# Reordered split matmuls and a cast-free modulated input in a two-layer hybrid backbone on one Trainium2 core

## The chip, the cores and the metric

The kernel runs on one core of one Trainium2 chip, in one launch. The core has TensorE (PE in the rows, its weight loads PEld), VectorE (DVE), ScalarE (ACT), GpSimd (POOL) and SyncE (SP), which issues the transfers. The metric is the device time of one launch in microseconds, lower is better.

## The reference

Two layers act on 256 latent and 256 context tokens with 1024 features. Each sub-layer normalises its input, scales and shifts it with a vector made from the conditioning (adaLN), runs a feed-forward network or a token mixer, and closes with a second normalisation over the residual sum. What matters here is

```
def _modulate(x, shift, scale):
    return (_ln(x) * (1.0 + scale) + shift).astype(x.dtype)
def _post_ln(x, y, g, b):
    z = ALPHA * x.astype(jnp.float32) + y.astype(jnp.float32)
    return (_ln(z) * g + b).astype(x.dtype)
def _ffn_sublayer(x, shift, scale, gate, w_in, w_out, g, b):
    a, u = jnp.split(_modulate(x, shift, scale) @ w_in, 2, axis=-1)
    y = (jax.nn.silu(a) * u) @ w_out
    return _post_ln(x, 0.5 * gate * y, g, b)
...
    for i in range(DEPTH):
        x = _ffn_sublayer(x, ...)            # and the context tokens
        h = _modulate(x, m[:, 3], m[:, 4])
        y, yc = even or odd mixer of h, hc   # odd: GLA, 4 heads, low-rank gate (16); HGRN2, 4 heads
        x = _post_ln(x, m[:, 5] * y, ...)
        x = _ffn_sublayer(x, ...)            # context too, unless it is the last layer
```

The hidden width of a feed-forward network is 2816. Layer 0 mixes with a Fourier transform and a long convolution (Hyena), layer 1 with two gated linear scans in chunks of 64. Everything is float32.

## The kernel before

**Tiles.** The 512 tokens are four tiles of 128: tiles 0 and 1 latent, 2 and 3 context. After the odd mixer only tiles 0 and 1 go on. A sub-layer's input lies in `hT`, transposed (features on the partitions), each value as a high and a low part in fp32r that together hold the float32 value. Weights are split likewise into whi and wlo (hi and lo where they lie in spare tiles). Every large product is three fp32r matmuls that add into one PSUM bank: high by high, high by low, low by high (`mm3`, L459 to L462). In the rows L460 is the first of the three, L461 has the low part of its left operand's partner or of the weight, L462 the other low part, depending on which operand is stationary.

**Weights.** Class `Stream` loads units of 512 KB with SP, casts the high part on ACT (L78) and subtracts for the low part on DVE (L79). `get()` hands out a unit and loads and splits two ahead of it; `split_to` splits up to a given unit at the place in program order where it stands. The order of each engine's instructions is the order of emission; nothing reorders them later.

**A close.** When a tile's output is complete, `close` runs: `post_ln` on DVE (gate, residual, statistics, z, x), `norm` (statistics on DVE, xn on ACT, L398), two sets of four transposes on PE (L411, tile ptr), and `to_hT` (L413) for each set g = 0, 1: four modulations into an fp32 tile hm, all four by DVE (L428) or all four by ACT (L430), then a cast of hm to the high part on ACT and a subtraction for the low part on DVE or POOL (both `split`, L226 and L227). These steps are a generator; `step`, `due` and `flush` advance it between the matmuls of the next tile or stage, at places set by numbers in the table `G0`. `tm_head` (L521) runs the first units of the next stage tile by tile while the last tiles still close. `tok_out` (L475) runs the output products; the last six units of a feed-forward output (`TAIL`) are done for one tile first, then for the other, so that the first tile's close lies under the second's matmuls.

**Start.** The first stage has an order of its own, the string `ORDER`; there `to_hT` reads the transposed input xT from SBUF, not ptr.

**Odd mixer.** `odd_mixer` (L1094) projects features with `fm_lat` (latent tokens only, tile ql) and `fm_unit` (L464), makes the low-rank gate as one such unit (tile pab, of which 32 rows are used), and runs `attend` (L1318): scores pF from products with 64 rows of contraction (L1331), a mask and a sum on DVE (am, L1342), then the output po from am (L1348) and from the states (L1351, 64 rows of contraction for GLA).

Of the kernel before, what the change touches and what calls it, by code (L numbers as in the profile page):

```python
# [9 lines left out]
F32 = mybir.dt.float32  # L10
# [118 lines left out]
def kernel(ctx: ExitStack, tc: tile.TileContext, a, out, stop=None):  # L129
# [283 lines left out]

    def to_hT(t, g, xn, l, m, pt=None, eng=None):

        s = t // 2
        if pt is None:
# [6 lines left out]
        for i in range(4):  # L424
            k = 4 * g + i
            sc, sh = modc[:, l, COL_OF[m + 1], s, k:k + 1], modc[:, l, COL_OF[m], s, k:k + 1]
            if eng[0]:
                dve.tensor_scalar(hm[:, i], pt[:, P * i:P * i + P], sc, sh, op0=ALU.mult, op1=ALU.add)  # L428
            else:
                act.activation(hm[:, i], pt[:, P * i:P * i + P], AF.Identity, bias=sh, scale=sc)  # L430
        yield
        dst = hT["all"][:, 4 * g:4 * g + 4, :, P * t:P * t + P]
        split(dst[:, :, 0], dst[:, :, 1], hm, gp if eng[1] else dve)
        yield

    pend = {}
# [26 lines left out]

    def fm_unit(o, view=lambda x: x):  # L464

        hi, lo = ws.get()
        for k in range(KD):
# [8 lines left out]
    def tok_out(lhs, nk, tiles, fill=None, tail=0, done=None, cuts=None, hmajor=False):  # L476


        cols = {t: [slice(0, 512), slice(512, 1024)] for t in tiles}
        if cuts:  # L480
            cols[tiles[-1]] = cuts
        y = {t: [PS("y")[:, 0:c.stop - c.start] for c in cols[t]] for t in tiles}

        def mm(t, w, k, i):
            hh, hl = lhs(k, t)
            c = cols[t][i]
            mm3(y[t][i], hh, hl, w[0][:, c], w[1][:, c], k == 0, k == nk - 1)

        for k in range(nk - tail):
            w = ws.get()  # L490
            for t in tiles:
                for i in range(len(cols[t])):
                    mm(t, w, k, i)
            if fill:
                fill(k)
        held = {}
        last = ws.pos + tail
        limit = last
        while limit < len(ws.units) and ws.units[limit][2]:
            limit += 1  # L500
        ks = range(nk - tail, nk)
        for n, t in enumerate(tiles if tail else ()):
            nc_ = range(len(cols[t]))
            for i, (h, k) in enumerate([(h, k) for h in nc_ for k in ks] if n or hmajor else [(h, k) for k in ks for h in nc_]):
                if k not in held:
                    held[k] = ws.get(limit)
                mm(t, held[k], k, h)
                if fill and i % 2 and i < 2 * len(ks):
                    fill(ks[i // 2])
            if done:  # L510
                done(t, y[t])
        return y

    def tm_mm(y, w, kp, t):

        for kk in range(2):
            k = 2 * kp + kk
            c = slice(512 * kk, 512 * kk + 512)
            x = hT[k][:, :, P * t:P * t + P]
            mm3(y, x[:, 0], x[:, 1], w[0][:, c], w[1][:, c], k == 0, k == KD - 1)  # L520

    def tm_head(tiles, done, n=1):

# [5 lines left out]
        for t in tiles:  # L529
# [4 lines left out]
            if nw:  # L534
                warm(nw)
            y = [PS("hd") for _ in range(n)]
            for u in range(4 * n):
                if u not in w:
                    w[u] = ws.get(limit)
                tm_mm(y[u // 4], w[u], u % 4, t)  # L540
                if u == g_(f"{k0}t{t}", 1) and todo:
                    run(todo)
                    todo = None
# [540 lines left out]

    def queue_odd():
        for f in range(17):
            ws.add(a["od_fm"][f], True, f < g_("SPN", 4), g_(f"qoi{f}", int(f in (1, 3, 4) or f > 5 and f % 2 == 1)))
# [6 lines left out]
    def odd_mixer():  # L1094
        ab_c = Q([P, 2, 2], name="abc")
        sy.dma_start(out=ab_c, in_=a["gla_a_b"])
        aup = H([32, 2, 256], name="aup")
        sy.dma_start(out=aup, in_=a["gla_up"])
        reset = []
        for d in range(2):  # L1100
# [20 lines left out]
        def fm_lat(n):  # L1121

            o = PS("ql")[:, 0:L]
            hi, lo = ws.get()
            for k in range(KD):
                x = hT[k][:, :, 0:L]
                mm3(o, hi[:, P * k:P * k + P], lo[:, P * k:P * k + P], x[:, 0], x[:, 1], k == 0, k == KD - 1)
            step(n)
            return o

# [19 lines left out]


        pab = PS("pab")
        fm_unit(pab)
        ab = H([32, T], name="ab")
        act.copy(ab, pab[0:32, :])
        E, U = [], []

        def gla_exp():
# [160 lines left out]
        def attend(j, tt):  # L1319
# [6 lines left out]
            for n, f, r, hd in lst:  # L1326
                for d in range(2):
                    qk, xx = QK[d, j], XX[d, j]
                    for c in (d, 1 - d):
                        kk = (qk if c == d else xx)[r, 1, f, P * tt:P * tt + P]  # L1330
                        pe.matmul(pa[d][n // 2][:, P * (n % 2) + 64 * c:P * (n % 2) + 64 * c + 64], lhsT=kk,  # L1331
                                  rhs=qk[r, 0, f, P * tt + 64 * c:P * tt + 64 * c + 64], start=True, stop=True)
            yield
            z = az[turn[0] % 2]
            turn[0] += 1
            for d in range(2):
# [6 lines left out]
            yield  # L1343
            yield
            po = [PS("po") for _ in range(nh // 2)]
            for n, f, r, hd in lst:
                oc = po[n // 2][:, P * (n % 2):P * (n % 2) + P]
                pe.matmul(oc, lhsT=am[:, P * n:P * n + P], rhs=v[tt][:, P * hd:P * hd + P], start=True, stop=False)  # L1348
                for d in range(2):
                    s = 0 if (d == 0) == (tt == 0) else 1  # L1350
                    pe.matmul(oc, lhsT=XX[d, j][r, 0, f, P * tt:P * tt + P], rhs=ST[d, j][r, s, f, :],  # L1351
                              start=False, stop=d == 1)
# [223 lines left out]
    def mixer_close(l, tiles, nxt):  # L1576
# [6 lines left out]
            return hT[k][:, 0, P * t:P * t + P], hT[k][:, 1, P * t:P * t + P]  # L1583

        def done(t, y):
            if t == tiles[-1]:
                ws.split_spare(ws.pos + g_(f"{k0}a", 3))
                flush()
            else:
                ws.split_spare(ws.pos + g_(f"{k0}A{t}", 0))  # L1590
                older.append(t - 1)
            if t == tiles[0]:
                key[0] = k0
# [9 lines left out]
        older = []  # L1603
        tok_out(lhs, KD, tiles, fill, KD, done, None, g_(f"{k0}h", 0))

    def dump_hT():
# [207 lines left out]
def lay_out(inputs):  # L1814
# [67 lines left out]
    o["gla_up"] = up  # L1882
# [29 lines left out]
```

## Time and profile before

| | us |
|---|---|
| median of 3 runs | 1823.25 (1817.42 to 1825.67) |
| profiled execution | 1824.63 |
| its span | 1822.80 |
| PE busy | 1744.2 (96%) |
| DVE busy | 1256.4 (69%) |
| ACT busy | 713.3 (39%) |
| POOL busy | 252.9 (14%) |

The profile is one execution. A row of the timeline gives start, duration, engine, line, operation, output and inputs by the program's names, shapes and count; in square brackets stands the engine's idle time just before, and what ended it. The view of waits adds such idle times by the waiting line and by what released it. The ends of matmuls are modelled, so in a run of matmuls the distance of their starts is the time that one takes.

### The profile page before, as it was taken

To read this page: it belongs to the slowest core of one execution; us is meant where nothing else is said; L and a number is where in the kernel's file an instruction comes from. 1 tells how busy PE (TensorE), PEld (TensorE's weight loads), DVE (VectorE), ACT (ScalarE), POOL (GpSimd) and SP (SyncE) were. 2 spreads that over 40 slices of the span, in tenths; PEclk is the share of its full clock that TensorE was granted. 3 is DMA by queue.
4 is the path that set the end of the run, shared out by engine and by line. 5 is a ranking of instruction groups with operands and counts; after the bars stand their busy time and mean duration, and the time that the engine had idled before them with its cause. 6 is when DMAs were issued, how large, how long until landed. Compare 5 with 4: busy or idle time off the path is not lost. (4 is left out here: it accounts for less than half of the span.)

```text
span 1822.8 us, 21896 instructions
## 1 busy us (share of the span) xinstructions
PE 1744.2 (96%) x8204; PEld 1414.9 (78%) x8204; DVE 1256.4 (69%) x1818; ACT 713.3 (39%) x1048; POOL 252.9 (14%) x273
## 2 busy tenths in 40 slices
PE   6999999998999999999999999999998999989998
PEld 5788888777766788888887788888877778767887
DVE  6788887676788677777477677733576594666755
ACT  5432233453323433323335423233355463444443
POOL 1223311011000111111001111111011241110000
PEclk9999999999999999999999999999999999889999
DMA  9645756653124055554655455435554223446664
GB/s 329 226 179 199 253 218 235 219 178 139 59 88 144 24 205 211 185 189 169 219 187 173 163 212 201 173 105 196 194 177 141 81 93 92 143 139 219 208 213 134
DMA packets 91498, 314.90 MB, mean 173 GB/s; under 512 B 10848, under 2 KB 11584, under 8 KB 91392
## 3 DMA queue, kind: packets, MB, share of 16 engines
q1 hardware_dynamic: 85952, 297.09, 47.0%
q0 software_dynamic: 4576, 15.91, 2.8%
q8 instruction: 64, 1.05, 0.2%
q10 hardware_dynamic: 864, 0.51, 0.1%
q14 instruction: 42, 0.34, 0.1%
HBM read 308.18 MB, written 4.24 MB: 171 GB/s over the span
## 5 line engine op out<-in xcount | busy, mean ns | idle before, releaser
L79 DVE TENSOR_TENSOR wlo<-raw,whi 128x1024 fp32r<-128x1024 f32 x332 | 415.3, 1254 | 321.6 <-ACT whi L78 321.4
L78 ACT CAST whi<-raw 128x1024 fp32r<-128x1024 f32 x332 | 346.8, 1051 | 338.5 <-PE y L462 122.8
L243 DVE SCALAR_TENSOR_TENSOR mt<-mraw,cb 128x1024 bf16<-128x1024 f32 x256 | 309.7, 1250 | 2.5 <-DMA mraw<-in_mod_w_dram 2.5
L462 PE MATMUL pu<-hT,wlo 128*128 128x512 f32 x576 | 224.7, 390 | 3.2 <-DVE wlo L79 3.2
L460 PE MATMUL pu<-hT,whi 128*128 128x512 f32 x576 | 225.7, 392 | 0.0
L461 PE MATMUL pu<-hT,whi 128*128 128x512 f32 x576 | 224.4, 390 | 0.0
L460 PE MATMUL pa<-hT,whi 128*128 128x512 f32 x480 | 187.8, 391 | 0.0
L462 PE MATMUL pa<-hT,wlo 128*128 128x512 f32 x480 | 187.1, 390 | 0.0
L461 PE MATMUL pa<-hT,whi 128*128 128x512 f32 x480 | 187.0, 390 | 0.0
L461 PE MATMUL y<-wlo,hh 128*128 128x512 f32 x468 | 183.2, 391 | 3.8 <-DVE wlo L79 3.8
L460 PE MATMUL y<-whi,hh 128*128 128x512 f32 x468 | 183.1, 391 | 0.0
L462 PE MATMUL y<-whi,hh 128*128 128x512 f32 x468 | 182.5, 390 | 0.0
L226 ACT CAST hh<-sa 128x256 fp32r<-128x256 f32 x120 | 42.8, 404 | 296.0 <-DVE sa L614 296.0
L227 POOL TENSOR_TENSOR hh<-sa,hh 128x256 fp32r<-128x256 f32 x120 | 86.3, 739 | 516.5 <-ACT hh L226 507.1
L462 PEld LDWEIGHTS pu<-hT,wlo 128*128 128x128 f32 x576 | 108.1, 188 | 26.6 <-DVE wlo L79 4.1
L460 PEld LDWEIGHTS pu<-hT,whi 128*128 128x128 f32 x576 | 108.1, 188 | 23.5 <-ACT hh L226 0.8
L461 PEld LDWEIGHTS pu<-hT,whi 128*128 128x128 f32 x576 | 108.2, 188 | 22.8 <-issue 0.5
L461 PEld LDWEIGHTS y<-wlo,hh 128*128 128x128 f32 x468 | 87.9, 188 | 24.9 <-DVE wlo L79 7.0
L460 PEld LDWEIGHTS pa<-hT,whi 128*128 128x128 f32 x480 | 90.1, 188 | 19.7 <-issue 0.9
L234 POOL TENSOR_TENSOR rstd<-rp,mhalf 128x1 f32<-128x1 f32 x42 | 35.4, 846 | 500.8 <-DVE rp L233 494.7
L462 PEld LDWEIGHTS pa<-hT,wlo 128*128 128x128 f32 x480 | 90.1, 188 | 18.8
L461 PEld LDWEIGHTS pa<-hT,whi 128*128 128x128 f32 x480 | 90.1, 188 | 18.5
(396 smaller groups left out, 3022.3 us busy)
## 6 DMA issues: line engine op xcount, KB each, us to landing
raw<-in_ffn_out_dram SPq DMA_DIRECT2D x154, 512.0 KB, 3.6
mraw<-in_mod_w_dram SPq DMA_DIRECT2D x144, 512.0 KB, 5.1
raw<-in_ffn_in_dram SPq DMA_DIRECT2D x120, 512.0 KB, 3.8
raw<-in_ffn_tm_dram SPq DMA_DIRECT2D x44, 512.0 KB, 4.2
raw<-in_od_fm_dram SPq DMA_DIRECT2D x17, 512.0 KB, 3.9
raw<-in_od_tm_dram SPq DMA_DIRECT2D x16, 512.0 KB, 3.3
raw<-in_ffn_head_dram SPq DMA_DIRECT2D x12, 512.0 KB, 4.3
raw<-in_ev_in_dram SPq DMA_DIRECT2D x12, 512.0 KB, 3.4
```

The costliest lines, as they stand in the source:

```text
L78: self.nc.scalar.copy(hi, w)
L79: self.nc.vector.tensor_tensor(lo, w, hi.bitcast(F32), op=ALU.subtract)
L226: act.copy(dst_hi, src)
L227: (lo_eng or dve).tensor_tensor(dst_lo, src, dst_hi.bitcast(F32), op=ALU.subtract)
L234: gp.tensor_tensor(dst, t, mhalf.to_broadcast([P, n]), op=ALU.pow)
L243: dve.scalar_tensor_tensor(H([P, D], BF16, "mt"), w, 1.0, cb[s], op0=ALU.mult, op1=ALU.mult, accum_out=acc[:, s, b:b + 1])
L460: pe.matmul(o, lhsT=wh, rhs=xh, start=start, stop=False)
L461: pe.matmul(o, lhsT=wh, rhs=xl, start=False, stop=False)
L462: pe.matmul(o, lhsT=wl, rhs=xh, start=False, stop=stop)
```

## The change

It has five parts.

1. The three products of a split matmul are no longer issued per k. `fm_unit`, `fm_lat`, `tok_out` (in blocks), `tm_mm` and `tm_head` issue a pass of high by high over all k (or units) first, then a pass with one low part, then a pass with the other. Their number is the same.
2. `to_hT` makes no cast. For each set of four columns one engine writes the modulated value straight into the fp32r high part (ACT for g = 0, DVE for g = 1), the other engine makes the same value in fp32 (hm), and DVE or POOL subtracts as before. Each of the 44 sets is thus modulated twice, eight instructions where there were four and a cast.
3. The low-rank gate (pab) takes its weight unsplit and runs as 16 fp32 matmuls of 32 columns that lie in four column groups, where 24 fp32r matmuls of 128 columns stood; the weight that follows is repeated four times to sum the groups.
4. `attend` issues its products so that those on the upper and the lower 64 rows stand next to each other and write different banks; for GLA there is no break between the scores and the mask.
5. The close of the odd mixer splits the next stage's weights during tile 0's output, by a list of unit numbers, not at the tiles' ends.

```
     def to_hT(t, g, xn, l, m, pt=None, eng=None):
...
+        dst = hT["all"][:, 4 * g:4 * g + 4, :, P * t:P * t + P]
+        def modulated(o, on_dve):
+            for i in range(4):
...
+                if on_dve:
+                    dve.tensor_scalar(o[:, i], pt[:, P * i:P * i + P], sc, sh, op0=ALU.mult, op1=ALU.add)
+                else:
+                    act.activation(o[:, i], pt[:, P * i:P * i + P], AF.Identity, bias=sh, scale=sc)
+        modulated(dst[:, :, 0], g)
+        yield
         hm = H([P, 4, P], name="hm")
...
-        split(dst[:, :, 0], dst[:, :, 1], hm, gp if eng[1] else dve)
+        modulated(hm, not g)
+        if not given:
+            yield
+        (gp if eng[1] else dve).tensor_tensor(dst[:, :, 1], hm, dst[:, :, 0].bitcast(F32), op=ALU.subtract)

     def fm_unit(o, view=lambda x: x):
-            mm3(o, hi[:, P * k:P * k + P], lo[:, P * k:P * k + P], view(hT[k][:, 0, :]), view(hT[k][:, 1, :]), k == 0, k == KD - 1)
+        for n, (a_, b_) in enumerate(((0, 0), (0, 1), (1, 0))):
+            for k in range(KD):
+                pe.matmul(o, lhsT=w[a_][:, P * k:P * k + P], rhs=view(hT[k][:, b_, :]), start=n + k == 0, stop=n == 2 and k == KD - 1)

     # tok_out
+        def block(todo):
+            for a_, b_ in ((0, 0), (1, 0), (0, 1)):
+                for t, w, k, i in todo:
+                    pe.matmul(y[t][i], lhsT=lhs(k, t)[a_], rhs=w[b_][:, cols[t][i]], start=k + a_ + b_ == 0, stop=k == nk - 1 and b_ == 1)

     # tm_mm (the first stage)
-            mm3(y, x[:, 0], x[:, 1], w[0][:, c], w[1][:, c], k == 0, k == KD - 1)
+            for n in range(2):
+                pe.matmul(y, lhsT=x[:, n], rhs=w[0][:, c], start=n + k == 0, stop=False)
+        for kk in range(2):
+            k = 2 * kp + kk
+            pe.matmul(y, lhsT=hT[k][:, 0, P * t:P * t + P], rhs=w[1][:, 512 * kk:512 * kk + 512], start=False, stop=k == KD - 1)

     # tm_head
+            order = ((0, 0), (1, 0), (0, 1)) if t == tiles[0] else ((0, 0), (0, 1), (1, 0))
+            for v in range(12 * n):
+                p_, u = divmod(v, 4 * n)

     # odd_mixer, pab
-        fm_unit(pab)
-        act.copy(ab, pab[0:32, :])
+        for n in range(2):
+            for k in range(KD):
+                j = k % 4
+                pe.matmul(pab[32 * j:32 * j + 32, :], lhsT=w[:, P * k:P * k + 32], rhs=hT[k][:, n, :].bitcast(F32),
+                          start=n == 0 and k < 4, stop=n == 1 and k >= 4, tile_position=(0, 32 * j))
+        act.copy(ab, pab)

     # mixer_close, fill(k)
+            if l and "y" not in seen:
+                ws.split_to(first + (4, 5, 7, 8, 9, 10, 11, 11)[k])
```

Three places in the order of instructions show what moves. The first is the start on DVE, where the modulation of the first tile's first set (hm from xT), the split of the first stage's second weight unit (lo from raw) and the low part of `hT` stand. Before:

```order
L1670 SCALAR_TENSOR_TENSOR modc<-pt_345,modb 128x2x4
L428 TENSOR_SCALAR hm_348<-xT_207,modc 128x128 x4
L79 TENSOR_TENSOR lo_354<-raw_164,hi_353 128x1024
L227 TENSOR_TENSOR hT_104<-hm_348,hT_104 128x4x128
L304 BN_STATS st_399<-x_175 128x6 x2
```

And now:

```order
L1717 SCALAR_TENSOR_TENSOR modc<-pt_345,modb 128x2x4
L79 TENSOR_TENSOR lo_353<-raw_164,hi_352 128x1024
L432 TENSOR_SCALAR hm_375<-xT_207,modc 128x128 x4
L442 TENSOR_TENSOR hT_104<-hm_375,hT_104 128x4x128
L304 BN_STATS st_402<-x_175 128x6 x2
```

The weight's subtraction has moved ahead of the modulation and of everything that follows it.

The second is ACT at the same place; modr is the row of conditioning that the first modulation waits for. Before:

```order
L1666 COPY modr_343<-pm_299 128x128
L78 CAST hi_353<-raw_164 128x1024
L226 CAST hT_104<-hm_348 128x4x128
L430 ACTIVATE hm_411<-xT_270,modc 128x128 x4
L226 CAST hT_104<-hm_411 128x4x128
```

And now:

```order
L1713 COPY modr_343<-pm_299 128x128
L434 ACTIVATE hT_104<-xT_207,modc 128x128 x4
L78 CAST hi_352<-raw_164 128x1024
L434 ACTIVATE hT_104<-xT_270,modc 128x128 x4
L226 CAST cf_102<-dft_231 128x256
```

The first set's high part is now written by ACT ahead of the weight's cast, for which DVE's subtraction waits.

The third is PE in `attend` for GLA, first token tile of the last pass: scores pF, products of the latent gate rc, outputs po. Before, one head's output and the next's:

```order
L1348 MATMUL po_12275<-vg_11879,am_12243 128x128
L1351 MATMUL po_12275<-st_12169,xx_11685 128x128
L1351 MATMUL po_12275<-st_12184,xx_11690 128x128
L1348 MATMUL po_12275<-vg_11879,am_12243 128x128
L1351 MATMUL po_12275<-st_12169,xx_11685 128x128
L1351 MATMUL po_12275<-st_12184,xx_11690 128x128
```

And now:

```order
L544 MATMUL rc_12346<-hi_12093,hT_10494 128x512 x4
L547 MATMUL rc_12346<-lo_12094,hT_10494 128x512 x2
L1388 MATMUL po_12353<-vg_11987,am_12342 128x128
L1388 MATMUL po_12354<-vg_11987,am_12342 128x128
L1392 MATMUL po_12353<-st_12277,xx_11793 128x128
L1392 MATMUL po_12354<-st_12277,xx_11793 128x128
L1392 MATMUL po_12353<-st_12292,xx_11798 128x128
L1392 MATMUL po_12354<-st_12292,xx_11798 128x128
```

Two heads now alternate, in two banks; the six products of rc ahead of them were twelve.

## Rows read from the trace of the kernel before

**Rows 1.** The page, busy time of each engine.

```profile
PE 1744.2 (96%) x8204; PEld 1414.9 (78%) x8204; DVE 1256.4 (69%) x1818; ACT 713.3 (39%) x1048; POOL 252.9 (14%) x273
```

**Rows 2.** Windows: stretch, length, busy time (count) of each engine, clock, DMA share, GB/s.

```profile
675.00:850.00 175.00, 175.00 (x774) 144.84 (x774) 131.07 (x192) 52.44 (x84) 23.93 (x34) 1.00 0.55 196
```

**Rows 3.** Waits of PE, whole span: us in total, times, longest.

```profile
PE ptr L411 <- ACT xn L398: 13.1, 10, 4.8
PE hd L460 <- ACT hT L226: 9.0, 6, 5.4
...
PE hd L461 <- DVE lo L79: 4.2, 3, 2.1
PE y L461 <- DVE wlo L79: 4.2, 8, 0.8
...
PE pab L461 <- DVE hT L227: 0.2, 1, 0.2
```

**Rows 4.** Groups of instructions by form: the cast of hm; busy, mean ns, idle before.

```profile
L226 ACT CAST hT<-hm 128x512 fp32r<-128x512 f32 x44 | 26.2, 632 | 17.2 <-DVE hm L428 17.0
```

**Rows 5.** Timeline of the start, 26 to 29 us.

```profile
26.13 1.05 ACT L78 CAST hi<-raw 128x1024 fp32r<-128x1024 f32 x1 [0.29 <-DMA raw<-in_ffn_head_dram]
...
26.56 1.12 DVE L428 TENSOR_SCALAR hm<-xT,modc 128x128 f32<-128x128 f32 x4
27.59 1.22 DVE L79 TENSOR_TENSOR lo<-raw,hi 128x1024 fp32r<-128x1024 f32 x1
27.71 0.62 ACT L226 CAST hT<-hm 128x512 fp32r<-128x512 f32 x1 [0.53 <-DVE hm L428]
28.23 1.65 ACT L430 ACTIVATE hm<-xT,modc 128x128 f32<-128x128 f32 x4
...
28.73 0.68 DVE L227 TENSOR_TENSOR hT<-hm,hT 128x512 fp32r<-128x512 f32 x1
```

**Rows 6.** Timeline, DVE and PE behind the first feed-forward close.

```profile
432.38 1.36 DVE L428 TENSOR_SCALAR hm<-ptr,modc 128x128 f32<-128x128 f32 x4
...
439.51 1.77 PE L411 MATMUL ptr<-ident,xn 128*128 128x128 f32 x8 [2.52 <-ACT xn L398]
```

**Rows 7.** Timeline of PE: a column-tiled product, plain fp32, ahead of the odd mixer.

```profile
34.67 0.65 PE L1661 MATMUL pm<-mraw,cst 128*32 128x128 f32 x16
...
516.09 1.88 PE L965 MATMUL po<-yf,raw 128*128 128x512 f32 x4
...
1380.96 1.33 PE L411 MATMUL ptr<-ident,xn 128*128 128x128 f32 x5 [4.84 <-ACT xn L398]
```

**Rows 8.** Groups by form, 1380 to 1410 us: one third of the low-rank gate.

```profile
L460 PE MATMUL pab<-hT,whi 128*128 128x512 f32 x8 | 3.2, 404 | 0.4 <-ACT hT L226 0.4
```

**Rows 9.** Timeline of PE in attend, GLA.

```profile
1554.38 0.43 PE L1331 MATMUL pF<-qk 64*128 64x64 f32 x2
...
1557.70 0.49 PE L460 MATMUL rc<-hi,hT 128*128 128x512 f32 x1
...
1562.83 0.46 PE L1348 MATMUL po<-vg,am 128*128 128x128 f32 x2 [2.10 <-DVE am L1342]
1563.22 1.17 PE L1351 MATMUL po<-st,xx 64*128 64x128 f32 x4
...
1569.71 0.63 PE L1331 MATMUL pF<-qk 64*128 64x64 f32 x2
...
1575.03 0.79 PE L460 MATMUL rc<-hi,hT 128*128 128x512 f32 x1
```

**Rows 10.** Timeline of PE and ACT behind the odd mixer's close.

```profile
1610.26 1.74 PE L411 MATMUL ptr<-ident,xn 128*128 128x128 f32 x8 [1.62 <-ACT xn L398]
...
1610.82 2.92 ACT L78 CAST hi<-raw 128x1024 fp32r<-128x1024 f32 x3
1613.65 1.49 ACT L430 ACTIVATE hm<-ptr,modc 128x128 f32<-128x128 f32 x4
...
1617.41 0.80 PE L460 MATMUL hd<-hi,hT 128*128 128x512 f32 x1 [5.41 <-ACT hT L226]
```

More of the change, by code (lines that the diff above doesn't have):

```diff
@@ L416, in to_hT @@
         s = t // 2
-        if pt is None:
+        given = pt is not None
+        if not given:
             pt = transposed(g, xn)
@@ L422, in to_hT @@
             eng = g_(f"{key[0]}e{t}{g}", odd), g_(f"{key[0]}l{t}{g}", odd)
-        hm = H([P, 4, P], name="hm")
[L424 to L432, printed above, removed]
-        split(dst[:, :, 0], dst[:, :, 1], hm, gp if eng[1] else dve)
+        dst = hT["all"][:, 4 * g:4 * g + 4, :, P * t:P * t + P]
+        def modulated(o, on_dve):
+            for i in range(4):
+                k = 4 * g + i
+                sc, sh = modc[:, l, COL_OF[m + 1], s, k:k + 1], modc[:, l, COL_OF[m], s, k:k + 1]
+                if on_dve:
[4 more added lines that the diff above has]
+        yield
+        hm = H([P, 4, P], name="hm")
+        modulated(hm, not g)
+        if not given:
+            yield
+        (gp if eng[1] else dve).tensor_tensor(dst[:, :, 1], hm, dst[:, :, 0].bitcast(F32), op=ALU.subtract)
         yield
@@ L503, in tok_out @@
             nc_ = range(len(cols[t]))
+            if not n and not hmajor:
+                for i, k in enumerate(ks):
+                    held[k] = ws.get(limit)
+                    block([(t, held[k], k, h) for h in nc_])
+                    if fill:
+                        fill(k)
+                if done:
+                    done(t, y[t])
+                continue
             for i, (h, k) in enumerate([(h, k) for h in nc_ for k in ks] if n or hmajor else [(h, k) for k in ks for h in nc_]):
@@ L536, in tm_head @@
             y = [PS("hd") for _ in range(n)]
-            for u in range(4 * n):
+            order = ((0, 0), (1, 0), (0, 1)) if t == tiles[0] else ((0, 0), (0, 1), (1, 0))
+            for v in range(12 * n):
+                p_, u = divmod(v, 4 * n)
                 if u not in w:
                     w[u] = ws.get(limit)
-                tm_mm(y[u // 4], w[u], u % 4, t)
+                for kk in range(2):
+                    k = 2 * (u % 4) + kk
+                    pe.matmul(y[u // 4], lhsT=hT[k][:, order[p_][0], P * t:P * t + P], rhs=w[u][order[p_][1]][:, 512 * kk:512 * kk + 512],
+                              start=p_ == 0 and k == 0, stop=p_ == 2 and k == KD - 1)
+                if v % 3 < 2:
+                    continue
+                u = v // 3
                 if u == g_(f"{k0}t{t}", 1) and todo:
@@ L1123, in fm_lat @@
             o = PS("ql")[:, 0:L]
[L1124 to L1127, printed above, removed]
+            w = ws.get()
+            for m, (a_, b_) in enumerate(((0, 0), (1, 0), (0, 1))):
+                for k in range(KD):
+                    pe.matmul(o, lhsT=w[a_][:, P * k:P * k + P], rhs=hT[k][:, b_, 0:L], start=m + k == 0, stop=m == 2 and k == KD - 1)
             step(n)
@@ L1152, in odd_mixer @@
         pab = PS("pab")
-        fm_unit(pab)
-        ab = H([32, T], name="ab")
-        act.copy(ab, pab[0:32, :])
+        w = ws.get()
+        for n in range(2):
+            for k in range(KD):
+                j = k % 4
+                pe.matmul(pab[32 * j:32 * j + 32, :], lhsT=w[:, P * k:P * k + 32], rhs=hT[k][:, n, :].bitcast(F32),
+                          start=n == 0 and k < 4, stop=n == 1 and k >= 4, tile_position=(0, 32 * j))
+        ab = H([P, T], name="ab")
+        act.copy(ab, pab)
         E, U = [], []
@@ L1325, in attend @@
             pa = [[PS("pF") for _ in range(nh // 2)] for _ in range(2)]
[L1326 to L1333, printed above, removed]
+            for d, c, (n, f, r, hd) in [(d, c, p) for f in range(2) for d in range(2) for c in (d, 1 - d) for p in lst if p[1] == f]:
+                qk, xx = QK[d, j], XX[d, j]
+                kk = (qk if c == d else xx)[r, 1, f, P * tt:P * tt + P]
+                pe.matmul(pa[d][n // 2][:, P * (n % 2) + 64 * c:P * (n % 2) + 64 * c + 64], lhsT=kk,
+                          rhs=qk[r, 0, f, P * tt + 64 * c:P * tt + 64 * c + 64], start=True, stop=True)
+            if j:
+                yield
             z = az[turn[0] % 2]
@@ L1585, in done @@
         def done(t, y):
+            seen["y"] = t
             if t == tiles[-1]:
-                ws.split_spare(ws.pos + g_(f"{k0}a", 3))
+                if not l:
+                    ws.split_spare(ws.pos + g_(f"{k0}a", 3))
                 flush()
-            else:
+            elif not l:
                 ws.split_spare(ws.pos + g_(f"{k0}A{t}", 0))
+            if t != tiles[-1]:
                 older.append(t - 1)
```

28 lines of the change are left out of this document (14 added, 14 removed).

## The prediction

> **What bounds the kernel now.** I read four views, in this order. The page's first part says that TensorE is busy 96% of the span, 1744.2 of 1822.80 us, and VectorE 69% [rows 1]; so the change can only touch the few per cent in which TensorE waits, or shorten TensorE's own work. The windows say where TensorE waits: in a stretch of the feed-forward main loop there is no idle time at all, 774 matmuls in 175.00 us, 0.226 us each [rows 2]. New pass orders gain nothing there. The view of waits then names what is left, at the seams between stages [rows 3]. Most of it falls on two steps: the transposes wait for the normalised tile (13.1 us), which the change does not shorten directly, and the products wait for the split input or the split weight. Fourteen rows of that view name hT, hi, lo or wlo as what came last, the first with 9.0 us, the last with 0.2; they sum to 32.5 us. That is the most that parts 1, 2 and 5 can take away. The timelines last, to see at each seam who is late next. VectorE is often that: at the seams it works without a gap, though it is idle 31% overall.
>
> **Part 2, no cast.** Before, a set of four modulations takes 1.36 us on VectorE [rows 6] or 1.49 on ScalarE [rows 10], the two sets of a tile side by side on two engines; the cast adds 0.63 [rows 4] and the subtraction 0.68 [rows 5]. So the high part is there 2.0 to 2.1 us after the transposes, the low part 2.7 to 2.8. After, the high part is there after 1.36 or 1.49, that is 0.6 earlier; the fp32 copy comes from the other engine, and in the new order it waits for the first, since both read one PSUM tile: 1.49 + 1.36 + 0.68 = 3.5, the low part 0.7 to 0.8 later. VectorE gets 44 sets where it had 24, 20 x 1.36 = 27 us more; ScalarE gets 44 where it had 20 and loses 44 casts of 0.63 [rows 4], 24 x 1.49 - 27.8 = 8 more. Both have room on average. What counts is where these stand in the queue.
>
> The Trainium skill (PSUM — Partial Sum Buffer, PSUM bank collisions raise a hardware error) says that two engines must not access one bank in the same partitions at the same time, reads against reads included. By that rule the 3.5 us stands; if the two readers could overlap, the low part would come 1.36 earlier, and the sum below would not move by more than 1, because the pass order covers the low part. No run here shows a collision.
>
> *Start: +4.0 (0 to +6.2).* Before, VectorE did hm at 26.56, the weight's lo at 27.59, the low part of hT at 28.73 to 29.41 [rows 5]. In the new order the weight's lo stands first on VectorE, and its cast on ScalarE stands behind the direct writes of the first set: 26.5 + 1.65 = 28.2, cast to 29.25, lo to 30.5, hm (1.12) to 31.6, subtraction to 32.2. The second product of the stage needs that low part: 2.8 us late. Behind it on VectorE wait the statistics of the next tiles and at least one more set of 1.12, hence 2.8 + 1.1 = 3.9, and with three sets more 6.2. The good end is 0, if a later wait for a transfer swallows it.
>
> *Closes of feed-forward networks: +1.4, and 0 for the rest.* At 432.38 VectorE runs from the modulation of tile 2 through x and the statistics to tile 3's norm without a break, and TensorE waits 2.52 us for that norm at 439.51 [rows 6]. Now a second set of 1.36 stands in that chain. The waits for lo and hT just before vanish but only lengthen this one. Ahead of the odd mixer the same kind of wait is 4.84 us [rows 7]; there the subtraction of two weights stands in the chain, and tile 2's sets come after it, so it stays. The close that feeds layer 0's second network into layer 1 I put at -0.5: waits for hT go there, and most of it comes back through the set that VectorE has more.
>
> **Part 1, passes.** *Output products: -3.4.* TensorE waits 4.2 us for wlo in eight places [rows 3], since the second matmul of a unit needs it. After, the first use comes eight matmuls later, 8 x 0.226 = 1.8 us, more than the longest of these waits (0.8). I take 3.4 and leave 0.8 for those in the last units, where the raw weight itself is late. The waits for lo in the tails stay: there a pass moves the need by three matmuls, 0.7 us, and what follows is the close's VectorE chain, so 0.
>
> *Feed-forward head behind the even mixer: -2.0.* Of the 4.2 us for lo [rows 3], one wait is 2.1, the other two, 2.1 together, stand here; with a pass over all units first, lo is needed four units later.
>
> *The other stages: -1.5.* In the even mixer VectorE is without a gap around the waits for wlo, so convolution work becomes the wait: 0. The odd mixer's hT and wlo waits (0.4 and 0.2 of them for the gate [rows 8, 3]) give 1.0, the last stage 0.5.
>
> **Part 3, the gate: -2.0 (-2.0 to +8.3).** Before, 24 matmuls at 0.226 = 5.4 us. After, 16 fp32 matmuls of 512 columns. Plain fp32 takes 1.88 us for four records, two matmuls, of 512 columns [rows 7], about 0.43 a record after the first; 32 records one after another are 13.7 us, a loss of 8.3. Four side by side are 3.4. A column-tiled product is in the trace: 16 records of 128 columns in 0.65 us [rows 7]; eight times that for 32 records of four times the columns would be 5.2, but the 0.65 includes the fill of one short product, and 16 serial records of 0.11 would take 1.7. So they do run side by side, and I take 3.4; a gain beyond it would need more than four at once, so -2.0 is the good end.
>
> **Part 4, attend: -4.0 (0 to -7).** The scores took 1557.70 - 1554.38 = 3.3 us in the first pass and 1575.03 - 1569.71 = 5.3 in the second, and the state products 1.17 for four, of eight such groups at 1.17 or 0.7 [rows 9], some 7. Products on the upper and lower 64 rows may run side by side: half of 3.3 + 5.3 + 7 is 7.8. But the first pass's gain is lost: the outputs waited 2.10 us for am on VectorE, and with half the scores' time and six products of rc fewer ahead they come to that wait earlier, while am comes only 0.6 earlier. That leaves 2.6 + 3.5 = 6.1 at best, 0 if nothing overlaps; I take two thirds, -4.0.
>
> **Part 5, the close of the odd mixer: -2.0 (0 to -5).** After the transposes (1610.26 to 1612.0) ScalarE first finished three weight casts (1610.82 to 1613.74), then hm, then the cast: TensorE stood 5.41 us [rows 10]. With these casts moved ahead, the first high part is there at 1612.0 + 1.49 = 1613.5, almost 4 us sooner. Yet the next tile's norm hangs on VectorE, which now has the weights' lo earlier and two sets per tile; I let half be given back. Queued behind the moved casts on ScalarE is the norm of tile 0 itself; if a cast waits for its load there, the 5.41 stays.
>
> **Sum.** +4.0 + 1.4 - 0.5 - 3.4 - 2.0 - 1.5 - 2.0 - 4.0 - 2.0 = -10.0 on the profiled 1824.63 (span 1822.80 and 1.83 around it), 1814.6. The median of the three runs lies 1.4 below the profiled one: **1813.2**.
>
> **Rivals.** *All waits go.* The 32.5 us vanish without a successor, the gate gives 2.0, attend 6.1, and the start loses nothing: -40.6, 1782.6 as a median. For it: TensorE is the bound everywhere else. Against: VectorE runs without a gap at several of the seams, as behind 432.38 [rows 6]. Partly true it gives anything from there to 1804.
> *VectorE is the bound at every seam.* Each removed wait returns as a wait for a norm or for am: +4.0 + 1.4 - 3.4 - 2.0 = 0.0, 1823.2. For it: the 13.1 us that the transposes wait for the norm, the largest row. Against: at the heads behind the mixers the waited-for step is ScalarE's.
> *Slower: the doubled sets in the closes.* In each of the three closes with four tiles, the sets of three tiles stand ahead of a next tile's norm; if VectorE has no gap there, three sets of 1.36 each are added to the path: 3 x 3 x 1.36 = 12.2, with the start's 4.0, less 3.4 and 2.0: +10.8, 1834.0. It decides from the point where tile 1's norm, not only tile 3's, is what TensorE waits for. For it: the 4.84 and 2.52 us. Against: the waits there stand at the last tiles only.
>
> **How the numbers follow.** A measurement of this kernel can tell about 0.5%, 9.1 us, from no change: 1814.1 and 1832.4 are the borders. My forecast has 0.50 (1804 to 1822), of which 0.31 lies below 1814.1 and 0.19 above; all waits go, 0.19; VectorE everywhere, 0.19; slower, 0.12. Faster 0.50, same 0.19 + 0.19 = 0.38, slower 0.12. The range 1793 to 1830 leaves out the slower case and some 0.08 of the first rival's far end.
>
> **What would show it.** Start: a wait of TensorE near 28.9 us for hT's low part of about 3 us. First close: the wait for tile 3's norm near 4 us. Waits for wlo in outputs gone from the view, the norm's row not below 13. The gate in 3 to 4 us. Scores in half the time, with a longer wait for am. Behind the odd mixer, TensorE's 5.41 us down to 2 or less. I am wrong if the norm's row falls well below 13 us (then nothing took the place of the waits), or if it grows beyond 20 (then VectorE's doubled sets decide).

## The result and the profile after

The changed kernel takes 1835.53 us, median of 4 runs (1833.81 to 1837.26); the kernel before took 1822.73 beside it (4 runs). The ratio on record is 1.0065, 95% interval 1.0048 to 1.0082 (the two medians alone give 1.0070): slower by some 0.7%, where 1813.2 was forecast. The profiled execution took 1833.81 with a span of 1832.00.

The page after, busy time of each engine (compare [rows 1]):

```profile
PE 1742.1 (95%) x8212; PEld 1411.6 (77%) x8212; DVE 1275.2 (70%) x1897; ACT 727.0 (40%) x1099; POOL 264.4 (14%) x273
```

TensorE works 2 us less and its span is 9 us longer, so its idle time grew by 11.3 us, from 78.6 to 89.9. VectorE has 19 us more work, ScalarE 14. The waits of TensorE, whole span: total, times, longest (compare [rows 3]):

```profile
PE ptr L411 <- ACT xn L398: 18.7, 7, 6.7
PE po L1388 <- DVE am L1381: 8.9, 2, 4.9
PE pt L935 <- DVE cv L921: 7.2, 3, 3.4
PE hd L544 <- DVE hT L442: 6.8, 3, 4.6
PE hd L571 <- ACT hi L78: 6.5, 6, 2.9
...
PE y L503 <- ACT whi L78: 3.2, 4, 1.7
```

The waits for wlo (the weight's low part) in outputs are gone, as forecast, but the outputs now wait 3.2 us for whi, the high part, for which no row stood before. The norm's row (xn) grew from 13.1 to 18.7 us and that of am (the masked scores) from 2.1 to 8.9; the row of cv (the even mixer's convolution) grew from 4.4 to 7.2, that of hi from 0.8 to 6.5, and VectorE's low part of hT from 1.1 to 6.8.

Where the 9.2 us grew is read from the start of one and the same instruction in both timelines. The table has the differences at each place, called offsets below, and how much came there:

| place (instruction) | before | after | difference | came here | forecast |
|---|---|---|---|---|---|
| start (transposes of ht in the first stage, pt) | 58.88 | 66.44 | +7.6 | +7.6 | +4.0 |
| close of first network (ptr) | 429.46 | 434.70 | +5.2 | -2.4 | |
| head and even mixer (pt) | 523.45 | 533.61 | +10.2 | +5.0 | +1.4 |
| its close, next head (pt) | 633.53 | 641.28 | +7.8 | -2.4 | -2.0 |
| second network, its close (ptr) | 963.57 | 969.14 | +5.6 | -2.2 | |
| head behind it (hd) | 1017.87 | 1025.41 | +7.5 | +1.9 | -0.5 |
| third network, odd mixer's head (pab) | 1400.69 | 1406.43 | +5.7 | -1.8 | -1.0, and -3.4 for the three outputs |
| gate (pf) | 1406.76 | 1410.00 | +3.2 | -2.5 | -2.0 |
| up to attend's end (pt) | 1584.47 | 1588.51 | +4.0 | +0.8 | -4.0 |
| odd mixer's close, head (pt) | 1637.55 | 1647.23 | +9.7 | +5.7 | -2.0 |
| end of span | 1822.80 | 1832.00 | +9.2 | -0.5 | -0.5 |

Most of what the change was to take away it did take away. Four places lost more than that. The first is the start. VectorE, GpSimd, ScalarE and TensorE at 29 to 42 us (compare [rows 5]):

```profile
29.21 1.23 DVE L79 TENSOR_TENSOR lo<-raw,hi 128x1024 fp32r<-128x1024 f32 x1 [2.65 <-ACT hi L78]
30.35 1.11 DVE L432 TENSOR_SCALAR hm<-xT,modc 128x128 f32<-128x128 f32 x4
31.50 0.69 DVE L442 TENSOR_TENSOR hT<-hm,hT 128x512 fp32r<-128x512 f32 x1
32.11 1.28 DVE L304 BATCH_NORM_STATS2 st<-x 128x6 f32<-128x512 f32 x2
...
34.94 1.06 DVE L432 TENSOR_SCALAR hm<-xT,modc 128x128 f32<-128x128 f32 x4
...
36.15 1.90 POOL L442 TENSOR_TENSOR hT<-hm,hT 128x512 fp32r<-128x512 f32 x1 [17.18 <-DVE hm L432]
38.02 1.29 POOL L227 TENSOR_TENSOR flo<-s,fhi 128x512 fp32r<-128x512 f32 x1
39.27 1.06 POOL L234 TENSOR_TENSOR rstd<-rp,mhalf 128x1 f32<-128x1 f32 x2
...
40.03 1.52 ACT L398 ACTIVATE xn<-x,nb,rstd 128x512 f32<-128x512 f32 x2 [7.97 <-DVE nb L395]
...
32.24 1.65 PE L544 MATMUL hd<-hi,hT 128*128 128x512 f32 x3 [4.60 <-DVE hT L442]
```

VectorE stood 2.65 us for the cast of a weight, with the first tile's copy queued behind it; the low part came at 32.2, as worked out, and TensorE had waited 4.60 us for it. What I missed comes after: the second set's copy stands behind the statistics, so GpSimd's subtraction starts at 36.15, the norm's own step (rstd) stands behind that on GpSimd, and ScalarE had stood 7.97 us when it made xn at 40.03.

The second place is the first close. VectorE and GpSimd, tile 2 (compare 432.38 in [rows 6]):

```profile
438.51 1.36 DVE L432 TENSOR_SCALAR hT<-ptr,modc 128x128 fp32r<-128x128 f32 x4
439.79 1.36 DVE L432 TENSOR_SCALAR hm<-ptr,modc 128x128 f32<-128x128 f32 x4
441.19 0.69 DVE L442 TENSOR_TENSOR hT<-hm,hT 128x512 fp32r<-128x512 f32 x1
441.80 2.28 DVE L353 SCALAR_TENSOR_TENSOR x<-z,rstd,lnb 128x1024 f32<-128x1024 f32 x1
...
441.56 1.44 POOL L442 TENSOR_TENSOR hT<-hm,hT 128x512 fp32r<-128x512 f32 x1 [4.12 <-ACT hm L434]
```

The same step x before:

```profile
434.26 1.27 DVE L353 SCALAR_TENSOR_TENSOR x<-z,rstd,lnb 128x1024 f32<-128x1024 f32 x1
```

And TensorE now:

```profile
448.05 1.33 PE L411 MATMUL ptr<-ident,xn 128*128 128x128 f32 x5 [6.70 <-ACT xn L398]
```

The second set is there with its 1.36 us, and x took 2.28 instead of 1.27 while GpSimd subtracted (441.56 to 443.00). The Trainium skill (SBUF — State Buffer, SBUF: two separate sides) has a rule for such a pair of engines, a lock held for a whole instruction. The row agrees: had x begun to run when GpSimd ended, it would have ended at 443.00 + 1.27 = 444.27, and it ended at 444.08. The wait grew from 2.52 to 6.70, that is by 4.2, but the transposes behind it came only 3.3 us later than the offset at the close's first ones (+8.5 against +5.2), since TensorE reached the wait sooner. The other 1.4 us of this row came in the even mixer, where the waits for cv stand.

The third is attend. TensorE, and VectorE in the second pass (compare [rows 9]):

```profile
1558.34 0.44 PE L1369 MATMUL pF<-qk 64*128 64x64 f32 x4
...
1560.27 1.21 PE L544 MATMUL rc<-hi,hT 128*128 128x512 f32 x4
...
1565.92 1.19 PE L1388 MATMUL po<-vg,am 128*128 128x128 f32 x4 [3.98 <-DVE am L1381]
...
1581.20 1.19 PE L1388 MATMUL po<-vg,am 128*128 128x128 f32 x4 [4.88 <-DVE am L1381]
...
1577.75 1.23 DVE L79 TENSOR_TENSOR wlo<-raw,whi 128x1024 fp32r<-128x1024 f32 x1 [2.02 <-ACT whi L78]
1578.90 1.43 DVE L1377 COPY_PREDICATED az<-masks,pF 128x256 f32<-128x256 int32 x4
```

The scores of the first pass went from 3.3 to 1.9 us, and all of it and more became waiting for am. In the second pass the mask (az) stood on VectorE behind the split of a weight, whose cast VectorE waited for. The fourth is the odd mixer's close. ScalarE and VectorE ahead of tile 0's z:

```profile
1599.55 1.05 ACT L78 CAST hi<-raw 128x1024 fp32r<-128x1024 f32 x1 [5.28 <-DMA raw<-in_ffn_tm_dram]
...
1603.32 1.23 DVE L79 TENSOR_TENSOR lo<-raw,hi 128x1024 fp32r<-128x1024 f32 x1 [1.46 <-ACT hi L78]
...
1606.19 0.68 DVE L331 TENSOR_TENSOR z<-y,gate 128x512 f32<-128x512 f32 x1
```

The moved casts wait for their transfers there, VectorE's subtractions for the casts, and the close for VectorE (z is the residual sum, its first step). TensorE's 5.41 us [rows 10] are gone (hd starts at 1618.84, right behind the transposes), but these transposes wait 3.92 us and a later unit 2.91:

```profile
1617.12 1.97 PE L411 MATMUL ptr<-ident,xn 128*128 128x128 f32 x8 [3.92 <-ACT xn L398]
...
1628.56 5.97 PE L571 MATMUL hd<-hi,hT 128*128 128x512 f32 x18 [2.91 <-ACT hi L78]
...
1638.88 1.36 PE L411 MATMUL ptr<-ident,xn 128*128 128x128 f32 x8 [2.09 <-ACT xn L398]
```

One more thing stands in the row of the core (span, mean granted clock), before and then after:

```profile
core 0: 1822.8 us, clock 0.984
```
```profile
core 0: 1832.0 us, clock 0.980
```

The clock is part of the loss. By the clock records of the two traces TensorE was granted the lower of its two levels (1.2 GHz, the upper is 2.4) for 58.2 us before and worked in 44.6 of them; after, for 72.4, and it worked in 55.1. The same score products took 5.3 us at the lower level and 2.8 at the upper (before and e7, below), a factor of 1.9, so I estimate the 10.5 us more of work at the lower level at some 5 us lost. The sum is then 11.3 more idle, some 5 from the clock, and some 7 of work saved. The new waits are among the places where the clock fell: with the 6.70 us wait inside, its mean in 438 to 452 us was 0.77 (the third value from the end), and in the last 4 us, when TensorE worked again, it was 0.50.

```profile
438.00:452.00 14.00, 7.30 (x29) 5.69 (x28) 10.26 (x24) 5.55 (x13) 1.99 (x2) 0.77 0.00 1
```

### The profile page after: what moved, and what is told of

It reads as the page before. It is cut to its first block, busy times and chain, and to the rows that moved or that the text cites. A ratio compares the mean times of both kernels' runs of the same rounds, so it can differ in the third digit from the quotient of the medians.

```text
span 1832.0 us, 22094 instructions
## 1 busy us (share of the span) xinstructions
PE 1742.1 (95%) x8212; PEld 1411.6 (77%) x8212; DVE 1275.2 (70%) x1897; ACT 727.0 (40%) x1099; POOL 264.4 (14%) x273
## 5 line engine op out<-in xcount | busy, mean ns | idle before, releaser
L478 PE MATMUL pu<-hT,whi 128*128 128x512 f32 x1152 | 274.3, 390 | 0.0
L503 PE MATMUL y<-whi,hh 128*128 128x512 f32 x924 | 229.9, 391 | 3.3 <-ACT whi L78 3.2
L478 PE MATMUL pa<-hT,whi 128*128 128x512 f32 x960 | 228.3, 390 | 0.0
L503 PEld LDWEIGHTS y<-whi,hh 128*128 128x128 f32 x924 | 172.6, 188 | 41.0 <-ACT whi L78 5.7
L478 PE MATMUL pu<-hT,wlo 128*128 128x512 f32 x576 | 142.4, 389 | 0.4 <-DVE wlo L79 0.4
L503 PE MATMUL y<-wlo,hh 128*128 128x512 f32 x462 | 124.1, 390 | 0.2
L478 PE MATMUL pa<-hT,wlo 128*128 128x512 f32 x480 | 118.5, 389 | 0.0
L478 PEld LDWEIGHTS pa<-hT,wlo 128*128 128x128 f32 x480 | 90.1, 188 | 18.7
L79 DVE TENSOR_TENSOR lo<-raw,hi 128x1024 fp32r<-128x1024 f32 x63 | 77.3, 1241 | 33.3 <-ACT hi L78 32.9
L78 ACT CAST hi<-raw 128x1024 fp32r<-128x1024 f32 x63 | 65.4, 1062 | 35.0 <-DMA raw<-in_ffn_out_dram 14.7
L571 PE MATMUL hd<-hi,hT 128*128 128x512 f32 x256 | 70.5, 424 | 6.5 <-ACT hi L78 6.5
```

What stands on the lines that cost most here:

```text
L78: self.nc.scalar.copy(hi, w)
L79: self.nc.vector.tensor_tensor(lo, w, hi.bitcast(F32), op=ALU.subtract)
L478: pe.matmul(o, lhsT=w[a_][:, P * k:P * k + P], rhs=view(hT[k][:, b_, :]), start=n + k == 0, stop=n == 2 and k == KD - 1)
L503: pe.matmul(y[t][i], lhsT=lhs(k, t)[a_], rhs=w[b_][:, cols[t][i]], start=k + a_ + b_ == 0, stop=k == nk - 1 and b_ == 1)
L571: pe.matmul(y[u // 4], lhsT=hT[k][:, order[p_][0], P * t:P * t + P], rhs=w[u][order[p_][1]][:, 512 * kk:512 * kk + 512], start=p_ == 0 and ...
```

## The experiments

Theory V: what part 2 doubles and part 5 and the missing break move stands on VectorE's or ScalarE's queue ahead of the next step on the path. Theory W: the passes themselves cost, as a head needs the high part of all its units at once. Times are medians in us; the ratio to the kernel before, run beside them, is given with its interval. That kernel's median went from 1822.2 to 1823.7 between the rounds of runs, so differences of 1 to 2 us across rounds are not resolved. The edits are shown shortened.

**e1_cast_back.** The changed kernel with the old `to_hT`.

```
-        modulated(dst[:, :, 0], g); ...; modulated(hm, not g); subtract
+        hm by one engine; split(dst[:, :, 0], dst[:, :, 1], hm, gp if eng[1] else dve)
```

> The changed kernel with the old making of the split input everywhere (four modulations by one engine, cast on ScalarE, subtraction); passes, gate, attend and moved splits stay. Theory V (VectorE's and ScalarE's queues: the second set of modulations and the moved splits stand ahead of steps on the path): the start's +6.2 us and some 3 to 4 of the first feed-forward close go, 1835.5 - 10 = about 1826 us, and the wait for tile 3's norm near 440 us is back to 3 us. Theory W (the passes themselves cost, since a head's first pass needs the high part of all its units at once): no part of the loss goes, 1833 or more, with the waits of hd for hi unchanged at 6 us.

1822.2 us, 0.9995 [0.9983, 1.0008]. Part 2 costs 13.3 us in the changed kernel, more than the whole loss, and without it the change is worth nothing. The wait near 440 us is back to 2.84:

```profile
440.73 1.97 PE L411 MATMUL ptr<-ident,xn 128*128 128x128 f32 x8 [2.84 <-ACT xn L398]
```

V's size was 10 and falls short by 3; as the cause of the loss W falls. That the passes cost nothing does not follow (see e7).

**e2_splits_back.** Part 5 undone (`mixer_close` as before).

```
-            if l and "y" not in seen:
-                ws.split_to(first + (4, 5, 7, 8, 9, 10, 11, 11)[k])
+                ws.split_spare(ws.pos + ...)   # in done, both layers
```

> The changed kernel with the odd mixer's close as before (part 5 undone). Theory V: the first tile's post-norm behind the odd mixer no longer waits behind two weight subtractions whose casts wait for a transfer; the step of +5.6 us in that close shrinks to about 0, 1835.5 - 5 = about 1830 us, though part of TensorE's old wait for the first high part (5.4 us before) returns. Theory W: the step is the passes' (the first pass of the head needs four units early), it stays, 1834 to 1837.

1832.5, 1.0054 [1.0038, 1.0071]. 3.0 less, but the intervals overlap with that of the changed kernel: part 5's price is not settled by this, but a gain of 2 us is unlikely. In the trace tile 0's transposes come 3.0 us earlier; then TensorE waits 2.53 for hT and 5.34 for tile 1's norm. From attend's end to the next head the offset still grows by 4.2 (from +4.2 to +8.4), where the changed kernel has +5.7: most of that row is there without part 5.

**e3_break_back.** The break in `attend` back; the pairs stay.

```
-            if j:
-                yield
+            yield
```

> The changed kernel with the break between the scores and the mask in attend put back for GLA; the paired products stay. Theory V: the mask stands on VectorE ahead of the weight subtractions that wait for a transfer, TensorE's two waits for am (8.9 us) fall to 3 to 5, 1835.5 - 4 = about 1831 us. Rival: with scores in half the time TensorE comes to the outputs early anyway, the waits stay at 8 or more, 1835.

1827.9, 1.0027 [1.0014, 1.004]: 7.7 us less. The waits for am in it:

```profile
PE po L1387 <- DVE am L1380: 5.3, 2, 2.6
```

Without the break the outputs come one step sooner: six products of rc, not twelve, cover the mask. The missing break lost more than I gave the pairs. The profiled execution, 1822.67, was the fastest of twelve, so the 7.7 is the medians' and the trace shows a lucky one: TensorE has the upper clock level from 1508 to 1604 us, through the end of attend.

**e4_start_cast.** The old `to_hT` in the first stage alone.

```
-        yield from to_hT(t, g, None, 0, 0, xT[t]...)
+        yield from to_hT_cast(t, g, None, 0, 0, xT[t]...)
```

> The changed kernel with the old making of the split input in the first stage only. Theory V: the offset of +6 to +7.6 us that the first 65 us build up falls to 1 or less and the rest of the trace keeps its steps, 1835.5 - 6 = about 1829.5 us. Rival (the start's loss is taken up by a later wait for transfers or for the next stage's weights): 1834 to 1836, the same offset after the first feed-forward network.

1830.3, 1.0038 [1.0022, 1.0054]: 5.2 less, about as expected. The offset at the start falls from +7.6 to +3.4, not to 1 or less.

**e5_only_nocast.** The kernel before with the new `to_hT`, nothing else.

> The kernel before with part 2 alone (direct high part, second modulation, no cast). Theory V (the doubled sets on VectorE and ScalarE are the loss, whatever the pass order): 1822.8 + 13 = about 1836 us, with the same +6 us at the start and +3 to 4 us at tile 3's norm near 440 us. Rival X (the sets only hurt together with the passes or with the moved splits): 1823 to 1828 us.

1836.3, 1.0073 [1.0049, 1.0096]: 12.6 over the kernel before. Part 2 costs the same with and without the passes; X falls. The places differ: without the passes the wait for tile 3's norm is only 3.56 (V expected 3 to 4 us on top of 2.52), and TensorE waits for the low part of hT instead, which comes late:

```profile
PE hd L471 <- DVE hT L442: 8.5, 7, 3.9
PE hd L471 <- POOL hT L442: 7.4, 4, 4.0
```

**e6_passes_gate_pairs.** Parts 1, 3 and the pairs of 4: e1 with e2's and e3's edits.

> Passes, gate and paired products of attend; the cast, the break in attend and the old close of the odd mixer are back. If the three undone parts add up (13.3 + 7.7 + 3.0 us, each measured by itself against the changed kernel): 1835.5 - 24.0 = 1811.5 us, 0.6% under the kernel before. If they overlap (each of them only lengthened another wait): 1818 us or more.

1812.6, 0.9943 [0.9923, 0.9962]. The three undone parts add up (1811.5 expected). This version is faster than both kernels; against the one before it is 0.6%.

**e7_passes_gate.** Parts 1 and 3 alone.

> Passes and gate alone; split input, attend and the odd mixer's close as before. By the trace offsets the closes of the feed-forward networks give 2 to 3 us in all, the head behind the even mixer 1.5, the gate 2.5, the rest 1: 1822.8 - 6 = about 1817 us. If every removed wait returns elsewhere but the gate's: 1820.5. The difference to the run with the paired products is what the pairs give: 4 by my forecast, 8 by the offsets of the run with the break.

1813.9, 0.9952 [0.9938, 0.9965]: 9.8 less than before. The pairs give 1.3 more (e6), which these intervals don't resolve.

Where the 9.8 came is another matter. Read at the places of the table, e7's offset is +2.6 at the start, +1.5 at the first close, +5.2 at the even mixer's pt, -0.7 at the gate's first product, -3.2 behind the gate, -12.3 at attend's end and -9.4 at the end of the span. Up to the gate the passes thus gained almost nothing: what they gained at the outputs and heads, the start and the stretch from the first close to the even mixer took back. The gate gave 2.5, and 9.2 came in attend, which is the old one in e7. In e6 attend is 10.6 shorter.

What differs there is the clock. Before, TensorE stood 2.10 us for am [rows 9] and then worked from 1563.3 to 1580.4 us at the lower level, clock 0.50. In e7 there was no such wait, since 3.4 us at the lower level happened to fall on the twelve products of rc ahead, which took 4.7 us and not 3.0, and am was ready at 1558.1, just ahead of their end; after that TensorE kept the upper level. Windows over attend, before, in e7 and in e6 (columns as in [rows 2], the clock third from the end):

```profile
1546.00:1586.00 40.00, 37.63 (x222) 31.44 (x221) 22.38 (x45) 16.22 (x28) 5.38 (x6) 0.79 0.49 160
```
```profile
1542.00:1575.00 33.00, 32.90 (x228) 27.18 (x227) 23.40 (x49) 17.51 (x32) 5.38 (x6) 0.95 0.57 187
```
```profile
1542.00:1570.00 28.00, 22.42 (x207) 18.38 (x206) 21.53 (x44) 14.91 (x25) 5.34 (x6) 1.00 0.51 171
```

The second scores from the same product on, the same work in the same order, took 1575.03 - 1569.71 = 5.3 us before [rows 9] and 1565.17 - 1562.34 = 2.8 in e7:

```profile
1562.34 0.38 PE L1362 MATMUL pF<-qk 64*128 64x64 f32 x2
...
1565.17 1.20 PE L535 MATMUL rc<-hi,hT 128*128 128x512 f32 x4
```

One trace of each kernel is kept, and the kernel before took from 1816.1 to 1828.3 us with mean clocks between 0.992 and 0.982, so these places can differ from one execution to the next; the 9.8 is the medians'. With the pairs (e6) the scores are shorter, but TensorE waits 5.6 us for am:

```profile
PE po L1378 <- DVE am L1371: 5.6, 2, 3.0
```

**e8_idle_set.** e1, and in the closes a second set by the other engine to a scratch tile, behind the first.

```
+        for i in range(0 if given else 4):   # same scale and shift, out = scratch
+            act.activation(o2, ...) if eng[0] else dve.tensor_scalar(o2, ...)
         yield
         split(...)
```

> The run with the cast back everywhere, and in the closes (not in the first stage) a second set of four modulations by the other engine behind the first, written to a scratch tile that nothing reads. It costs the engines' time of part 2 without its dependence. If the queue time is the loss in the closes: 1822.2 + 13.3 - 5.2 = about 1830 us. If the loss is that the low part now waits for the two engines in turn: 1822 to 1825 us.

1891.1, 1.0377 [1.0353, 1.0401]: a miss on both theories. The scratch set stands ahead of the cast on ScalarE and waits there for VectorE's set; the high part is late at eight places (TensorE waits 25.9 us for hT from ScalarE). It does not measure queue time alone.

**e9_casts_behind.** e6 with `"m1a": 0` for 4: three weight casts behind tile 0's modulation.

> Passes, gate and paired products (1812.6 us) with one number of the order table changed: behind the odd mixer the three weight casts stand behind the first tile's modulation on ScalarE, not ahead of it. Theory V (what stands ahead of a tile's chain on its engine's queue is the price): the wait of 5.8 us for the first high part falls to about 3, the second tile's norm comes about 3 us sooner, 1810 us. Rival (the first pass needs the weights' high parts of all units at once, so the casts are late instead): 1812 to 1814 us with a longer wait for hi.

1815.5, 0.9959 [0.9945, 0.9974]: 2.9 over e6, which the two intervals don't resolve. V's 1810 fails, and the rival's wait is there, though the time lies above its range too. The wait for the first high part fell from 5.8 to 2.10, but hi is late instead, 3.44 and 1.35:

```profile
1600.57 4.63 PE L562 MATMUL hd<-hi,hT 128*128 128x512 f32 x10 [2.10 <-ACT hT L226]
1608.64 1.22 PE L562 MATMUL hd<-hi,hT 128*128 128x512 f32 x2 [3.44 <-ACT hi L78]
1611.22 7.61 PE L562 MATMUL hd<-hi,hT 128*128 128x512 f32 x20 [1.35 <-ACT hi L78]
```

**e11_start_order.** The changed kernel, only the first stage's order string edited.

```
-t00 w f R t00 F x x p2 p3 t10 t10
+t00 t00 w f R F x x t10 t10 p2 p3
```

> The changed kernel with the tokens of the first stage's order string exchanged: the fp32 copy and low part of the first tile's two sets stand on VectorE ahead of the weight's subtraction and of the next tiles' statistics. The doubled work stays. If the order alone makes the start's loss (4.6 us of wait for the low part near 32 us): that wait falls to 1 to 2, 1835.5 - 3 = about 1832.5 us. If the doubled work makes it: 1835 us, the wait only moves to the next tiles' norm.

1830.3, 1.0045 [1.003, 1.006]: 5.2 less by the medians, as much as the cast back in the start gave. The offset at the start is +3.0, where e1 with the old `to_hT` has +2.6: part 2's loss at the start is the order, not the doubled work, and the rest is there without part 2. The wait for the low part:

```profile
28.37 1.65 PE L544 MATMUL hd<-hi,hT 128*128 128x512 f32 x3 [1.26 <-DVE hT L442]
```

**e12_idle_set_late.** e8 with the scratch set behind the low part's subtraction.

> The run with the cast back everywhere, and in the closes a second set of four modulations by the other engine to a scratch tile that nothing reads, now behind the low part's subtraction, so that it stands ahead of no step of its own set. It costs only queue time. If queue time is the loss in the closes (8 us: 13.3 less the start's 5.2): 1828 to 1831 us. If the loss is that the low part waits for two engines in turn: 1822 to 1824 us.

1855.7, 1.0178 [1.0156, 1.0201]: 33.5 over e1, four times what I expected. The sign fits queue time, the size doesn't. Here the casts are still on ScalarE, and a scratch set also waits for the other engine; that this makes the size is argued and not shown, so whether queue time alone is the price in the closes stays open. At the first close it moves the way of the changed kernel, 4.57 us where e1 has 2.84 and the changed kernel 6.70:

```profile
445.04 1.97 PE L411 MATMUL ptr<-ident,xn 128*128 128x128 f32 x8 [4.57 <-ACT xn L398]
```

**e13_tile2_cast.** e11, with the old `to_hT` for tile 2 in every close.

```
+        make = to_hT_cast if t == 2 else to_hT
+        tr = zipped(make(t, 0, xn[t], *nxt), make(t, 1, xn[t], *nxt))
```

> The run with the start's order mended (1830.3 us), and tile 2 alone of every close makes its split input as before, with a cast. If the loss in the closes is the second set that stands on VectorE ahead of tile 3's norm: the wait near 440 us falls from 6.7 to about 3 us, with some 1 us more at the other two closes of four tiles, 1830.3 - 4 = about 1826 us. If it is spread over all tiles (tiles 0 and 1 delay the next tile as much): 1828 to 1830 us.

1826.4, 1.0021 [1.0012, 1.0029]: 4.0 less than e11. TensorE's wait for tile 3's norm, 6.69 in e11:

```profile
441.50 1.82 PE L411 MATMUL ptr<-ident,xn 128*128 128x128 f32 x8 [2.95 <-ACT xn L398]
```

## Why the prediction was wrong, point by point

By the experiments the parts add up. Part 2 costs 13.3 us (e1), the missing break 7.7 (e3), part 5 3.0 (e2, not resolved), the pairs give 1.3 (e7 to e6, not resolved), parts 1 and 3 give 9.8 (e7): +12.9, and +12.8 was measured. The forecast had +4.9, nothing, -2.0, -4.0 and -8.9. So the steps that failed are part 2's size, attend and part 5.

- **The gate held, part 1 by luck.** I gave the outputs 3.4, the head behind the even mixer 2.0, the other stages 1.5, the gate 2.0, together 8.9; e7 measured 9.8. The gate alone took 3.57 us (1406.43 to 1410.00), a gain of 2.5 by the offsets. But the rest of the 9.8 is not where I put it: up to the gate e7's trace gained 0.7, as losses that I put at nothing (2.6 at the start, waits for cv and for whi) took back the outputs' and the head's gains, and 9.2 came in attend, where these parts had no term. That the sum fits is luck.
- **Part 2, +1.4 for the closes, was mis-sized.** The mechanism at tile 3's norm was right, its size there 1.36 against a wait that grew by 4.2 and 3.3 us lost. Tile 2's sets cost 4.0 (e13); all closes together 13.3 - 5.2 = 8.1. I had let the other two closes and tiles 0 and 1 go at -0.5 and 0. Where the remaining 4 lies is not settled.
- **The start, +4.0, was low.** e4 and e11 both measure 5.2. The working to 32.2 us was exact; what it left out is GpSimd's queue, where the norm's rstd waits behind the late subtraction. With e11's order part 2 costs next to nothing there. By the offsets the start lost 7.6; 2.6 of it stays with the old `to_hT` (e1, e7), where TensorE's clock was 0.65 in 27 to 30 us and 0.50 in 30 to 33 us (e7), and 1.00 before.
- **Attend, -4.0, failed as a step, twice.** First, I read the 5.3 us of the second scores and the 1.17 us of the state products as the work's length. They are the same work at the lower clock: e7, with the old attend, has 2.8 and 0.71. So part of what I hoped to gain was the clock's and not the pairs' to give. Second, I noted that six products of rc cover the mask where twelve did, but took only the first pass's gain off for that. The missing break costs 7.7 (e3). The pairs' own gain is at most a few us (e7 to e6, 1.3, not resolved): in half the time TensorE reaches a mask that VectorE has no sooner.
- **Part 5, -2.0, gained nothing.** By e2 it costs about 3, not resolved. The offsets have +5.7 at its place, of which +4.2 is there in e2 without it. I named the risk (a cast that waits for its load) and did not price it.
- **The sum left out the clock.** Every added wait was counted at its length. The work at the lower level grew by 10.5 us, an estimated 5 us of time.
- **The slower rival** (1834.0) met the time. Its mechanism, doubled sets ahead of a next norm, is part 2's, 13.3 us with the start, where it had 16.2; but it lacked the break and part 5, and it put the gain of parts 1 and 3 at 5.4 where e7 has 9.8. These cancel, so that its number was met is partly luck.
- **The signs.** I named a norm's row well below 13 or beyond 20 us as the signs of being wrong. It came to 18.7, so neither showed, and the forecast was wrong all the same: the row sees one kind of wait only.

## What to carry to other kernels

A step that is shortened for one engine by giving another engine work must be placed in that engine's queue: look at what stands behind it there, not at how idle the engine is on average. A break in a generator is an order too; what covers a wait must be counted in instructions before it is taken away. Before a stretch is halved on paper, look at the clock that it ran at. Try the parts of a change one at a time: here two of five gave nearly all the gain, and the others took it back and more. And read where a gain came, not only its sum.

## What the runs showed of the hardware that was not expected

- Plain fp32 matmuls of 32 columns in four column groups ran at 32 records in 3.57 us, 0.11 a record, against about 0.43 for a record of 128 columns alone [rows 7]: four at once, nearly in full.
- Scores on two row halves took 1.9 us for 32 records where they had taken 3.3, a factor of 1.7, not 2.
- A wait of 2.10 us was followed by 17.1 us of TensorE at the lower clock, without a pause in its work (before, 1563.3 to 1580.4 us, clock 0.50). By the two levels that is an estimated 8 us, four times the wait.
